# One order of matmuls for every block of a weight product

## The chip, the cores and the metric

The kernel runs on one core of a Trainium2 chip. The metric is the device time of one execution in microseconds (us), as the median of several timed runs. Beside the timed runs there is one profiled execution with a trace, from which all durations of single instructions come.

## The reference, cut to what matters

One layer of a decoder for 256 tokens of 2048 features, all in float32. The input is normalised, projected to ten pieces, and goes through two mixers side by side: latent attention with 16 heads, and a short causal convolution with gates. Both are projected, merged by sigmoid gates, and projected once more.

```python
h = _rmsnorm(x, pre_norm_g)
proj = jnp.einsum('bsd,de->bse', h, w_in)
(q_a, c_kv, k_rope, z_mla, c_in, b_gate, c_gate, z_conv, g_mla, g_conv) = jnp.split(proj, cuts, axis=-1)
q = jnp.einsum('bsr,re->bse', _rmsnorm(q_a, q_a_norm_g), w_q_b)
kv = jnp.einsum('bsr,re->bse', _rmsnorm(c_kv, kv_a_norm_g), w_kv_b)
...
attn = _causal_mla_attention(q_nope, q_rope, k_nope, k_rope, v)
attn = attn.reshape(b, s, MLA_WIDTH) * jax.nn.silu(z_mla)
y_mla = jnp.einsum('bse,ed->bsd', attn, w_o_mla)
u = c_gate * c_in
conv = sum(conv_w[k] * u_pad[:, k:k + s] for k in range(CONV_K))
y_conv = jnp.einsum('bse,ed->bsd', b_gate * conv * jax.nn.silu(z_conv), w_o_conv)
merged = jax.nn.sigmoid(g_mla) * y_mla + jax.nn.sigmoid(g_conv) * y_conv
out = jnp.einsum('bsd,de->bse', merged, w_out)
x = x + _rmsnorm(out, post_norm_g)
```

## The kernel before

Every float32 weight and every activation is split into two parts of 12 bits (float32r): a high part and the rest. A product of two such operands is taken as three products: high x high, high x rest, rest x high.

**The stream of weights.** `plan` lists units of [128, 2048] in the order of their use. `load_raw` brings a unit in on SP's queue, three units ahead. `split_unit` cuts it in two halves of 1024 columns; for each, `split_act` (L202 to L204) lets ScalarE write the high part `whi` and VectorE subtract it from the raw values into the rest `wlo`. There are five buffers of each. `take` hands out pieces of a unit, and before that calls `ahead`, which issues the loads and splits to come.

**The weight products.** The activations lie as `both`: 256 tokens' high parts and, beside them, their 256 rests, so one matmul with 512 columns multiplies a high weight part by both, and one with 256 columns multiplies the weight's rest by the high parts. This pair is `halves` (L196 to L200). It adds up over the contracted features in one PSUM bank of [128, 512]; at the end of a block `whole` (L311) adds the bank's two halves: ScalarE copies the right half out (`half`), and VectorE adds it to the left. A block of `project` (L320) has 16 pairs, a block of `narrow` (L430) 4. Four banks (`mm`) take turns. The products of two activations (scores, values) and the last projection (`out_products`, with `product`, L189) don't use `halves`.

**The stages.** First the latent query `qa` (four banks side by side, each pair goes to each bank in turn), then the latent keys and values `ckv` in four blocks, then `kr`. Beside them run the norms: the sums of squares go through a matmul with ones (`ss_...`, L289), GpSimd raises the mean to the power -1/2 (`r_...`, L295), VectorE puts it on a diagonal (`dg_...`, L299), and another matmul spreads it over all partitions (`rb_...`, L306). GpSimd (POOL) also computes the rotary angles in a long row of small steps (`tables`, L334 to L350). Then come 16 heads: in each, five blocks (`z`, `cg`, `ci`, `b`, `c`) beside the attention of the head, and the queries, keys and values (`qn`, `kn`, `qr`, `vv`) of the next two heads. Then 16 rounds of the output stage, with two gate blocks `g` and two blocks `y` each, and at last the shared output projection, its norm, the residual and the store.

**What sets the order.** Each engine has one queue. The code gives an order of issue, but the kernel is built with a scheduler that orders the instructions of each engine by its own estimate of their times:

```python
    with tile.TileContext(nc, schedule_with_timeline_sim=True) as tc:
        tile_layer(tc, *args)
```

Of the kernel before, what the change touches and what calls it, by code (L numbers as in the profile page):

```python
# [19 lines left out]
S = 256  # L20
NT = S // P
D = 2048
# [13 lines left out]
UNIT = 2048  # L36
HALF = UNIT // 2

# Column blocks of the packed small parameters: per-feature vectors, feature 128 k + p at [p, k].
PV = {}  # L40
_at = 0
for _name, _n in (
# [35 lines left out]
def tile_layer(ctx: ExitStack, tc: tile.TileContext, xt, x, pos, pvec, post_g, wqa, wi, wkr, wqk, wrv, wom, woc, wout, out):  # L78
# [3 lines left out]
    wpool = ctx.enter_context(tc.tile_pool(name="wpool", bufs=1))  # L82
    psum = ctx.enter_context(tc.tile_pool(name="psum", bufs=1, space=PSUM))

# [1 line left out]
    plan = []  # L86

    def add(ap, width=UNIT):
# [14 lines left out]
    order = []  # L103
    for h in range(H):
        g, second = divmod(h, HG)
# [81 lines left out]
        return psum.tile([P, 512], F32, name=name, tag=tag, bufs=bufs)  # L187

    def product(ps, a, b, first, last):  # L189
        # ps += a.T @ b, each operand in its two parts  # L190
        (ah, al), (bh, bl) = a, b
        nc.tensor.matmul(ps, ah, bh, start=first, stop=False)  # L192
        nc.tensor.matmul(ps, ah, bl, start=False, stop=False)  # L193
        nc.tensor.matmul(ps, al, bh, start=False, stop=last)  # L194

    def halves(ps, w, both, first, last):  # L196
        # both [128, 512]: 256 columns' parts side by side; ps[:, :256] + ps[:, 256:] += w.T @ columns
        order = ((w[0], 2 * S), (w[1], S)) if first else ((w[1], S), (w[0], 2 * S))
        for i, (a, n) in enumerate(order):
            nc.tensor.matmul(ps[:, :n], a, both[:, :n], start=first and i == 0, stop=last and i == 1)  # L200

    def split_act(hi, lo, src):  # L202
        nc.scalar.activation(hi, src, AF.Copy)  # L203
        nc.vector.tensor_tensor(lo, src, hi.bitcast(F32), op=ALU.subtract)  # L204

# [1 line left out]
    pv = const.tile([P, PV_N], F32, name="pv")  # L207
    nc.scalar.dma_start(out=pv[:, :], in_=pvec)

# [21 lines left out]
    cos_t = const.tile([P, S], F32, name="cos_t")  # L231
    sin_t = const.tile([P, S], F32, name="sin_t")

# [1 line left out]
    main = ctx.enter_context(ExitStack())  # L235
    hp = main.enter_context(tc.tile_pool(name="hp", bufs=1))
    x_both = hp.tile([P, KD, 2 * S], F32R, name="x_both")
# [7 lines left out]
    qa = bp.tile([P, KR, 2 * S], F32R, name="qa")  # L245
    ckv = bp.tile([P, KR, 2 * S], F32R, name="ckv")
    kr = bp.tile([P, 2, S], F32R, name="kr")
    # before the heads fill them: x, then the rotary angles; the latents, squares, sums, row norms
    xs = at_f
    angles = [at_f[:, H - 1 - i, :] for i in range(5)]  # L250
    lat_f = {"qa": cv_f[:, :KR, :], "ckv": cv_f[:, KR : 2 * KR, :]}
# [5 lines left out]
    def temp(name, shape=(P, S), dt=F32, bufs=2, tag=None):  # L257
        return bp.tile(list(shape), dt, name=name, tag=tag or name.rstrip("0123456789_"), bufs=bufs)

# [1 line left out]
    def x_chunk(i, j, pieces):  # L261
        n = 4 // pieces
        ks = slice(4 * i + n * j, 4 * i + n * (j + 1))
# [7 lines left out]
        )  # L271
        return a, b

# [1 line left out]
    def squares(name, chunks):  # L275
        # [128, 256]: sums of squares over the features of each partition
        acc = acc_f[name]
        for i, src in enumerate(chunks):
            nc.scalar.activation(sq_f, src, AF.Square)
            part = temp("f")[:, :] if i else acc  # L280
            nc.vector.reduce_sum(part, sq_f.rearrange("p k t -> p t k"), axis=mybir.AxisListType.X)
            if i:
                nc.vector.tensor_tensor(acc, acc, part, op=ALU.add)
        return acc
# [22 lines left out]
        nc.scalar.activation(r, rb[:, :S], AF.Copy)  # L307
        return r

# [1 line left out]
    def whole(dst, ps):  # L311
        # dst = ps[:, :256] + ps[:, 256:]
        t = temp("half")
        nc.scalar.activation(t[:, :], ps[:, S:], AF.Copy)
        nc.vector.tensor_tensor(dst, ps[:, :S], t[:, :], op=ALU.add)
# [8 lines left out]
            halves(ps, w(k, P), both[:, k, :], k == 0, k == KD - 1)  # L324
        return ps

# [1 line left out]
    def tables():  # L328
        pi = angles[4].bitcast(I32)
        nc.scalar.dma_start(out=pi, in_=pos.to_broadcast([P, S]))  # L330
        y, n1, n2, r = angles[:4]
        v = nc.gpsimd
        nc.vector.tensor_copy(y[:, :], pi)
        v.tensor_scalar(r[:, :], y[:, :], col("freq"), None, op0=ALU.mult)  # L334

        def less(r, n, c):
            # r -= n c, the product exact
            v.tensor_scalar(y[:, :], n[:, :], c, None, op0=ALU.mult)  # L338
            v.tensor_tensor(r[:, :], r[:, :], y[:, :], op=ALU.subtract)

        inv = 1.0 / (2.0 * math.pi)
        big, small = 1.5 * 2.0**38, 1.5 * 2.0**23
        v.tensor_scalar(y[:, :], r[:, :], inv, None, op0=ALU.mult)
        v.tensor_scalar(n1[:, :], y[:, :], big, big, op0=ALU.add, op1=ALU.subtract)
        v.tensor_tensor(n2[:, :], y[:, :], n1[:, :], op=ALU.subtract)
        v.tensor_scalar(n2[:, :], n2[:, :], small, small, op0=ALU.add, op1=ALU.subtract)
        for w, c in TERMS:
            less(r, (n1, n2)[w], c)
        v.tensor_scalar(n1[:, :], r[:, :], inv, small, op0=ALU.mult, op1=ALU.add)
        v.tensor_scalar(n1[:, :], n1[:, :], small, None, op0=ALU.subtract)  # L350
        for c in COARSE:
            less(r, n1, c)
        lim = float(np.nextafter(np.float32(math.pi), np.float32(0)))
        nc.vector.tensor_scalar(r[:, :], r[:, :], lim, -lim, op0=ALU.min, op1=ALU.max)
        nc.vector.scalar_tensor_tensor(y[:, :], r[:, :], -1.0, r[:, :], op0=ALU.mult, op1=ALU.max)
        nc.scalar.activation(n2[:, :], r[:, :], AF.Sin)
        nc.scalar.activation(cos_t[:, :], y[:, :], AF.Sin, bias=hpi[:, :], scale=-1.0)
        nc.vector.tensor_scalar(sin_t[:, :], n2[:, :], col("sign"), None, op0=ALU.mult)

    def rope(src, dst):  # L360
        # rows 0-31, 64-95: first halves; 32-63, 96-127: second halves
        a, b = temp("rp_a", bufs=1), temp("rp_b", bufs=1)
        nc.vector.tensor_tensor(a[:, :], src, cos_t[:, :], op=ALU.mult)
        for q in range(4):
            i, o = slice(32 * q, 32 * q + 32), slice(32 * (q ^ 1), 32 * (q ^ 1) + 32)
            nc.vector.tensor_tensor(b[o, :], src[i, :], sin_t[i, :], op=ALU.mult)
        nc.vector.tensor_tensor(dst, a[:, :], b[:, :], op=ALU.add)

# [1 line left out]
    def times_rows(dst):  # L370
        n = dst.shape[1]
        nc.vector.tensor_tensor(dst, dst, r_x[:, :].unsqueeze(1).to_broadcast([P, n, S]), op=ALU.mult)
# [48 lines left out]
        rope(kr_f, kr_f)  # L421
        split_act(kr[:, 0, :], kr[:, 1, :], kr_f)

# [1 line left out]
    def pair(name, shape, bufs=1):  # L425
        return [temp(f"{name}_{n}", shape, F32R, bufs, tag=f"{name}_{n}") for n in ("hi", "lo")]

# [22 lines left out]
    def group_b(g):  # L450
        qr, vv = temp("qr", (P, HG, S), F32R), pair("vv", (P, NT, HG * DV), 2)
        w = take(u_grp[g][1])
        f = narrow(f"qr{g}", w, 0, qa)
        rope(f[:, :], f[:, :])
        for j in range(HG):
            # both parts in one contraction: the first where the head's rows are, the second in the other rows
            own, other = (slice(DR * i, DR * i + DR) for i in (j, 1 - j))
            split_act(qr[own, j, :], qr[other, j, :], f[own, :])
        for t in range(NT):
            ps = bank(f"vv{g}_{t}", **({} if g else {"tag": ("o", "tp")[t], "bufs": 1}))  # L460
            for k in range(KR):
                c = [ckv[:, k, o + t * P : o + (t + 1) * P] for o in (0, S)]
                product(ps[:, :S], c, w(2 + k, HG * DV), k == 0, k == KR - 1)
            split_act(vv[0][:, t, :], vv[1][:, t, :], ps[:, :S])
        groups[g] += [qr, vv]

    def scores(h):
        # queries 0-127 by keys 0-127, in two addends; queries 128-255 by keys 0-255
        qn, kn, qr, _ = groups[h // HG]
        j = h % HG  # L470
        sc = bank(f"sc{h}", tag="sc", bufs=1)
# [32 lines left out]
        return p  # L504

    def turn(h, p):
        # keys 0-127 by queries 0-255; keys 128-255 by queries 128-255
        tp = bank(f"tp{h}", tag="tp", bufs=1)
        for b in range(3):
            nc.tensor.transpose(tp[:, b * P : (b + 1) * P], p[:, b * P : (b + 1) * P], ident[:, :])  # L510
        pt = temp("pt", (P, 2, 3 * P), F32R, 1)
        split_act(pt[:, 0, :], pt[:, 1, :], tp[:, : 3 * P])
        return pt
# [21 lines left out]
        return s  # L535

    def values_next(h):
        # this head's share of the next group
        g, second = divmod(h, HG)
        if g + 1 < NG:  # L540
            (group_b if second else group_a)(g + 1)
# [40 lines left out]
            values_next(h)  # L582
            values(h, turn(h, p), sz)

# [1 line left out]
    bstack.close()  # L586
    cp = main.enter_context(tc.tile_pool(name="cp", bufs=1))
    bp = cp
# [24 lines left out]
        split_act(m_both[:, d, :S], m_both[:, d, S:], m[0][:, :])  # L613
    main.close()

# [1 line left out]
    op = ctx.enter_context(tc.tile_pool(name="op", bufs=1))  # L617
    xr = op.tile([P, NT, D], F32, name="xr")
    og = op.tile([P, NT, D], F32, name="og")
# [21 lines left out]
    part = op.tile([P, NT], F32, name="part")  # L641

    def row_norm(t):
        # part: the squares of the first three blocks of columns, over D, plus eps
        ss = op.tile([P, 1], F32, name=f"fss{t}")
        nc.vector.scalar_tensor_tensor(
            ss[:, :], ssq[:, t, 3:4], 1.0 / D, part[:, t : t + 1], op0=ALU.mult, op1=ALU.add
# [30 lines left out]


def _cols(w):  # L680
    # [K, n 128] -> [n, 128, K]: block n's rows of 128 contracted features, side by side
    k, n = w.shape
    return np.ascontiguousarray(
        w.reshape(k // P, P, n // P, P).transpose(2, 1, 0, 3)
    ).reshape(n // P, P, k)
# [82 lines left out]
```

## Time and profile before

| | us |
|---|---|
| timed runs, median of 3 | 1084.33 |
| timed runs, lowest and highest | 1084.27, 1085.43 |
| profiled execution, span from its first to its last instruction | 1083.1 |
| TensorE matmuls busy in it | 1064.9 |
| VectorE busy | 785.4 |
| ScalarE busy | 599.1 |
| GpSimd busy | 47.4 |

The page gives the profiled execution by its span alone; what lies around the span is in the timed runs and not in the profile. Matmuls overlap in the records, and their ends are modelled, so the time that one matmul costs in a stream is read from the start of it to the start of the next. A line such as L200 is that of a helper, so groups are told apart by the names of the tiles: `g<-x_both,whi` writes the bank `g` from the activations and a high weight part. The idle time of TensorE is in the list of waits, by the matmul that waited and what released it.

### The profile page before, as it was taken

The page shows a single profiled execution, that of the slowest core. Times are in us where ns is not written, and L with a number is a line of the kernel's source. Part 1 is how long each engine was busy: PE and PEld are TensorE (multiplying, and loading weights), DVE is VectorE, ACT ScalarE, POOL GpSimd, SP SyncE. Part 2 cuts the span into 40 slices and gives each one's busy share as a digit, 9 for nine tenths or more (in the row PEclk, how much of TensorE's full clock was granted, in tenths as well). Part 3 has the DMA queues.
Part 4 walks back from the last instruction along what each step waited for, and adds up shares of the span by engine and source line. Part 5 has one row for each costly group of instructions (what it writes and reads, how often), then busy time and mean ns, then how long its engine had stood idle before and what let it go on. Part 6 is the DMA issues. An engine that isn't in the chain of part 4 may idle for free.

```text
span 1083.1 us, 15562 instructions
## 1 busy us (share of the span) xinstructions
PE 1064.9 (98%) x6056; PEld 927.0 (86%) x6056; DVE 785.4 (73%) x1260; ACT 599.1 (55%) x937; POOL 47.4 (4%) x70
## 2 busy tenths in 40 slices
PE   8999999999999999999999999999999999999997
PEld 7877888888888888888888888888888888888885
DVE  6899897877877878778787786656566565665562
ACT  7557566665656656566555674444444444444450
POOL 0591000000000000000000000000000000000000
PEclk9999999999999999999999999999999999999999
DMA  8544554454545545545545545555555555556652
GB/s 312 203 162 156 185 177 165 160 211 165 194 160 181 194 154 193 189 153 188 177 179 179 187 161 198 193 194 180 177 188 194 194 179 178 188 194 264 218 179 78
DMA packets 31610, 199.89 MB, mean 185 GB/s; under 512 B 3632, under 2 KB 5296, under 8 KB 9264
## 3 DMA queue, kind: packets, MB, share of 16 engines
q1 hardware_dynamic: 30960, 195.57, 51.2%
q10 hardware_dynamic: 576, 3.31, 0.8%
q8 instruction: 48, 0.79, 0.3%
q14 instruction: 26, 0.21, 0.0%
HBM read 196.78 MB, written 2.10 MB: 184 GB/s over the span
## 4 chain that ended last, share of the span: by engine, by line
PE 90%; DVE 3%; POOL 3%; issue 2%; DMA 1%; ACT 0%; SPq 0%; POOLq 0%; DVEq 0%; ACTq 0%
PE y L200 17%; PE g L200 17%; PE c L200 8%; PE b L200 8%; PE cg L200 8%; PE z L200 8%; PE ci L200 8%; PE out L194 2%; PE out L193 2%; PE out L192 2%; PE kn L200 2%; PE qn L200 2%; DMA raw<-wqa_dram 1%; POOL at_f L338 1%; PE qr L200 1%
## 5 line engine op out<-in xcount | busy, mean ns | idle before, releaser
L204 DVE TENSOR_TENSOR wlo<-raw,whi 128x1024 fp32r<-128x1024 f32 (+1 forms) x372 | 448.0, 1208 | 150.7 <-ACT whi L203 141.7
L203 ACT ACTIVATE whi<-raw 128x1024 fp32r<-128x1024 f32 (+1 forms) x374 | 386.2, 1035 | 202.3 <-PE y L200 39.3
L200 PE MATMUL g<-x_both,whi 128*128 128x512 f32 x512 | 181.1, 398 | 0.0
L200 PE MATMUL g<-x_both,wlo 128*128 128x256 f32 x512 | 138.6, 281 | 0.0
L200 PEld LDWEIGHTS g<-x_both,whi 128*128 128x128 f32 x512 | 95.3, 188 | 21.0
L200 PEld LDWEIGHTS g<-x_both,wlo 128*128 128x128 f32 x512 | 96.7, 189 | 2.7
L200 PE MATMUL b<-x_both,whi 128*128 128x512 f32 x256 | 94.3, 406 | 0.0
L200 PE MATMUL y<-at_both,whi 128*128 128x512 f32 x256 | 91.8, 398 | 0.0
L200 PE MATMUL cg<-x_both,whi 128*128 128x512 f32 x256 | 91.8, 398 | 0.0
L200 PE MATMUL y<-cv_both,whi 128*128 128x512 f32 x256 | 91.8, 398 | 0.0
L200 PE MATMUL ci<-x_both,whi 128*128 128x512 f32 x256 | 91.4, 397 | 0.0
L200 PE MATMUL c<-x_both,whi 128*128 128x512 f32 x256 | 91.2, 395 | 0.0
L200 PE MATMUL z<-x_both,whi 128*128 128x512 f32 x256 | 91.1, 396 | 0.0
L200 PE MATMUL b<-x_both,wlo 128*128 128x256 f32 x256 | 69.7, 283 | 0.0
L200 PE MATMUL y<-at_both,wlo 128*128 128x256 f32 x256 | 69.3, 281 | 0.0
L200 PE MATMUL y<-cv_both,wlo 128*128 128x256 f32 x256 | 69.3, 281 | 0.0
L200 PE MATMUL cg<-x_both,wlo 128*128 128x256 f32 x256 | 69.3, 281 | 0.0
L200 PE MATMUL c<-x_both,wlo 128*128 128x256 f32 x256 | 69.2, 281 | 0.0
L200 PE MATMUL z<-x_both,wlo 128*128 128x256 f32 x256 | 69.1, 280 | 0.0
L200 PE MATMUL ci<-x_both,wlo 128*128 128x256 f32 x256 | 68.8, 279 | 0.0
L200 PEld LDWEIGHTS b<-x_both,whi 128*128 128x128 f32 x256 | 48.7, 190 | 10.0
L200 PEld LDWEIGHTS y<-cv_both,whi 128*128 128x128 f32 x256 | 48.2, 188 | 10.5
(235 smaller groups left out, 1979.8 us busy)
## 6 DMA issues: line engine op xcount, KB each, us to landing
raw<-wi_dram SPq DMA_DIRECT2D x116, 1024.0 KB, 4.8
raw<-wom_dram SPq DMA_DIRECT2D x16, 1024.0 KB, 4.8
raw<-woc_dram SPq DMA_DIRECT2D x16, 1024.0 KB, 4.8
raw<-wout_dram SPq DMA_DIRECT2D x16, 1024.0 KB, 4.9
raw<-wqk_dram SPq DMA_DIRECT2D x8, 1024.0 KB, 4.8
raw<-wrv_dram SPq DMA_DIRECT2D x8, 768.0 KB, 4.3
raw<-wqa_dram SPq DMA_DIRECT2D x8, 256.0 KB, 4.5
raw<-wqa_dram SPq DMA_DIRECT2D x4, 512.0 KB, 8.0
```

The lines of the kernel that those rows point to most:

```text
L192: nc.tensor.matmul(ps, ah, bh, start=first, stop=False)
L193: nc.tensor.matmul(ps, ah, bl, start=False, stop=False)
L194: nc.tensor.matmul(ps, al, bh, start=False, stop=last)
L200: nc.tensor.matmul(ps[:, :n], a, both[:, :n], start=first and i == 0, stop=last and i == 1)
L203: nc.scalar.activation(hi, src, AF.Copy)
L204: nc.vector.tensor_tensor(lo, src, hi.bitcast(F32), op=ALU.subtract)
L338: v.tensor_scalar(y[:, :], n[:, :], c, None, op0=ALU.mult)
```

## The change

Only `halves` changes. Before, the first pair of a block has the matmul of 512 columns first and that of 256 second, and all later pairs have them the other way round. After, every pair has 512 first and 256 second. The first matmul of a block must in both cases be the one of 512 columns, since it starts the accumulation in the whole bank; the last is now one of 256 columns, where it was one of 512.

```diff
     def halves(ps, w, both, first, last):
-        # both [128, 512]: 256 columns' parts side by side; ps[:, :256] + ps[:, 256:] += w.T @ columns
-        order = ((w[0], 2 * S), (w[1], S)) if first else ((w[1], S), (w[0], 2 * S))
-        for i, (a, n) in enumerate(order):
+
+        for i, (a, n) in enumerate(((w[0], 2 * S), (w[1], S))):
             nc.tensor.matmul(ps[:, :n], a, both[:, :n], start=first and i == 0, stop=last and i == 1)
```

The changed file also has its comments taken out, and all lines behind this place stand one line higher (L200 becomes L199). No other code differs, but the scheduler places the instructions of all engines anew.

## The prediction

> **What bounds the kernel now.** I read the page from the top: the busy shares, then the chain that ended last.
>
> ```profile
> span 1083.1 us, 15562 instructions
> PE 1064.9 (98%) x6056; PEld 927.0 (86%) x6056; DVE 785.4 (73%) x1260; ACT 599.1 (55%) x937; POOL 47.4 (4%) x70
> PE 90%; DVE 3%; POOL 3%; issue 2%; DMA 1%; ACT 0%; SPq 0%; POOLq 0%; DVEq 0%; ACTq 0%
> ```
>
> TensorE matmuls are 98% of the span and 90% of the chain. The busy share alone would not prove that TensorE works without pause, since ends of matmuls are modelled. So I went to the waits of TensorE, which is the complete list (us in total, times, longest):
>
> ```profile
> PE rb_qa L306 <- DVE dg_qa L299: 2.6, 1, 2.6
> PE rb_ckv L306 <- DVE dg_ckv L299: 2.6, 1, 2.6
> PE qa L200 <- DVE wlo L204: 2.1, 2, 1.1
> PE idle L230 <- POOL ones L217: 1.1, 1, 1.1
> PE vv L192 <- DVE cg L315: 0.7, 1, 0.7
> PE rb_x L306 <- DVE dg_x L299: 0.6, 1, 0.6
> PE qa L200 <- ACT whi L203: 0.4, 1, 0.4
> ```
>
> Seven groups, 10.1 us in all, and every one of them lies in the first 140 us (the last is vv; its place, 138.66 us, is in the chain row quoted below). From there to the end nothing makes TensorE wait. So two questions decide the change: does a block of matmuls take another time in the new order, and what happens to the waits of the first 140 us.
>
> **The change, part by part.** *The matmul stream.* A block of `project` or `narrow` is a run of pairs, one matmul of 512 columns with the first part of a weight (whi) and one of 256 with the second (wlo). Before, the first pair is 512, 256 and all later pairs 256, 512; so at the seam of two blocks two 512s stand together, and then two 256s. After, 512 and 256 alternate throughout. No matmul is added or removed. Here is one block and its two seams in the timeline (start, duration):
>
> ```profile
> 901.83 0.62 PE L200 MATMUL g<-x_both,whi 128*128 128x512 f32 x2
> 902.30 0.40 PE L200 MATMUL g<-x_both,wlo 128*128 128x256 f32 x2
> 902.53 0.40 PE L200 MATMUL g<-x_both,whi 128*128 128x512 f32 x1
> 902.76 0.28 PE L200 MATMUL g<-x_both,wlo 128*128 128x256 f32 x1
> 902.88 0.40 PE L200 MATMUL g<-x_both,whi 128*128 128x512 f32 x1
> ...
> 907.48 0.40 PE L200 MATMUL g<-x_both,whi 128*128 128x512 f32 x1
> 907.72 0.39 PE L200 MATMUL y<-at_both,whi 128*128 128x512 f32 x1
> 907.94 0.40 PE L200 MATMUL y<-at_both,wlo 128*128 128x256 f32 x2
> 908.18 0.40 PE L200 MATMUL y<-at_both,whi 128*128 128x512 f32 x1
> ```
>
> Durations overlap, so I use starts. Alternating: from 902.53 to 907.48 are 14 pairs, 4.95 us, 0.3536 us a pair; a 256 takes 0.12 (902.76 to 902.88) and a 512 0.23 to 0.24. Around the seam: 512, 512, 256, 256 take 902.53 - 901.83 = 0.70 us, and again 908.18 - 907.48 = 0.70. The same four in alternation are two pairs, 0.707 us. So a seam costs 0.007 us more after, and rounding of the starts to 0.01 could make that zero. The blocks are 4 qa, 4 ckv, 16 x 5 in the heads, 16 x 4 in the output stage, and 8 x 5 short ones for queries and keys: 192 seams at most. That is 192 x 0.007 = 1.3 us at one end, 0 at the other; many seams in the heads are interrupted by score matmuls anyway, so I take the middle, **+0.7 us**.
>
> *The norm of the latents in the head of the kernel.* The scheduler places instructions by its own estimate, so a new order of matmuls moves other work. The programs as built differ in the heads' first stretch thus (count of weight matmuls before each norm matmul):
>
> ```
>             before                              after
> ss_qa       after 8 of z                        after 21 of z
> rb_qa       after 23 of cg                      after 9 of ci      (18 later)
> ss_ckv      after 13 of ci                      after 31 of ci     (18 later)
> rb_ckv      after 20 of b                       after 5 of c       (17 later)
> r_qa  on POOL                                   two table steps later
> r_ckv on POOL                                   one table step later, the last one
> ```
>
> rb_qa and rb_ckv are the two largest waits above. The timeline of TensorE and of POOL around them:
>
> ```profile
> 70.96 0.68 PE L306 MATMUL rb_qa<-dg_qa,ones 128*128 128x128 f32 x4 [2.62 <-DVE dg_qa L299]
> 85.40 0.68 PE L306 MATMUL rb_ckv<-dg_ckv,ones 128*128 128x128 f32 x4 [2.60 <-DVE dg_ckv L299]
> ```
> ```profile
> 70.01 0.72 POOL L339 TENSOR_TENSOR at_f<-at_f 128x256 f32<-128x256 f32 x1
> 70.82 0.90 POOL L338 TENSOR_SCALAR at_f<-at_f 128x256 f32<-128x256 f32 x1
> 71.81 0.74 POOL L339 TENSOR_TENSOR at_f<-at_f 128x256 f32<-128x256 f32 x1
> ...
> 81.30 0.91 POOL L338 TENSOR_SCALAR at_f<-at_f 128x256 f32<-128x256 f32 x1
> 82.85 1.63 POOL L295 TENSOR_TENSOR r_ckv<-v_ckv,mhalf 128x2 f32<-128x2 f32 x1 [0.65 <-DVE v_ckv L293]
> 84.45 0.72 POOL L339 TENSOR_TENSOR at_f<-at_f 128x256 f32<-128x256 f32 x1
> ```
>
> POOL works through the rotary tables in a row, and r_qa and r_ckv are queued among them. At rb_qa: the weights' 18 matmuls that now go ahead are 9 pairs, 9 x 0.3536 = 3.2 us of cover; r_qa comes two table steps later, 71.81 - 70.01 = 1.8 us. The wait of 2.6 becomes 2.6 + 1.8 - 3.2 = 1.2. At rb_ckv: one table step ahead of r_ckv takes from 82.21 (81.30 + 0.91) to about 83.1, against a start at 82.85 now: 0.25 us later, since POOL waited 0.65 there. Over both waits TensorE idled 5.2 us; after, 17 matmuls more (3.0 us) are done by then: 5.2 + 0.25 - 3.0 = 2.5. **A lead of 2.7 us** when rb_ckv is over.
>
> *The clock behind the wait.* The stretches just behind rb_ckv, with the granted clock in the sixth value:
>
> ```profile
> 86.00:88.00 2.00, 2.00 (x9) 1.75 (x9) 2.00 (x4) 1.73 (x3) 0.00 (x0) 0.60 0.99 418
> 88.00:90.00 2.00, 2.00 (x8) 1.62 (x7) 1.96 (x6) 1.25 (x5) 0.00 (x0) 0.55 0.03 12
> ```
>
> At 0.60 and 0.55, these 4 us did 1.2 + 1.1 = 2.3 us of full-clock work: 1.7 us lost, after an idle time of 2.6; the same wait at rb_qa was not followed by it. A wait cut to at most 2.5, probably shared between two places, need not bring it: up to **1.7 us** more, a lead of 4.4.
> By the Trainium skill ("TensorE: Matmul & The Clock Gate", Part 1) the gate closes after an idle window of about 3.4 us, free-running. By that rule 2.6 us should not have closed it, and here it did; the measurement decides. By the rule alone the 1.7 us would be lost in neither kernel, and the lead would be 2.7.
>
> *What is late next.* The lead is worth something only if the operands are there. VectorE (third value):
>
> ```profile
> 70.00:80.00 10.00, 9.04 (x55) 8.07 (x56) 9.89 (x15) 4.69 (x10) 9.15 (x12) 1.00 0.48 174
> 80.00:90.00 10.00, 7.41 (x35) 6.15 (x35) 9.35 (x20) 5.94 (x11) 4.43 (x4) 0.83 0.30 107
> 90.00:100.00 10.00, 10.00 (x62) 8.89 (x62) 9.96 (x22) 6.40 (x13) 0.10 (x1) 1.00 0.45 145
> 100.00:120.00 20.00, 20.00 (x122) 17.70 (x121) 19.80 (x39) 15.44 (x29) 0.00 (x0) 1.00 0.61 218
> ```
> ```profile
> 97.40 0.42 DVE L204 TENSOR_TENSOR ckv<-cv_f,ckv 128x256 fp32r<-128x256 f32 x1
> ```
> ```profile
> 98.45 1.17 PE kn L200 x7
> 138.66 0.39 PE vv L192
> ```
>
> Between 70 and 120 us VectorE is idle for 0.11 + 0.65 + 0.04 + 0.20 = 1.0 us in all. It makes the second parts of the weights, the parts of ckv that the key product kn reads (ready at 97.82, read from 98.45), and the drains of the banks, and none of that work goes away. So TensorE can be earlier by that 1.0 us, at most by 1.0 + 0.6 (the 0.6 between 97.82 and 98.45), and the rest of the lead turns into waits at kn, at the first scores or at head 1's z. I take **-1.0 us** (ends 0 and -1.6). The wait of 0.7 at vv (138.66) then meets a VectorE that has caught up or not: 0 to -0.7, I take **-0.4**.
>
> *At nothing.* The qa blocks now ask for whi first, which may shorten the 2.1 us of waits for wlo; but rb_qa and rb_ckv come from POOL's table chain, not from TensorE's start, so what is gained there idles at rb_qa (if that cover fell, up to -2.1). A whi buffer comes free one 256 earlier and a wlo buffer one 512 later, 0.24 us; no row shows VectorE waiting for TensorE, and this stays far from mattering. The new order also groups ScalarE's work so that 21 table loads stand in the program instead of 33:
>
> ```profile
> L533 ACT ACT_TABLE_LOAD x16 | 20.5, 1283 | 0.3
> ```
>
> 12 x 1.28 = 15 us of ScalarE saved, on an engine that is 55% busy and 0% of the chain. SP's order of transfers is the same in both.
>
> *Sum.* +0.7 - 1.0 - 0.4 = -0.7 us, so the profiled execution's 1083.1 becomes 1082.4. The median of the timed runs, 1084.33, lies 1.2 us above the span, which I take for what lies around it; 1084.33 - 0.7 = **1083.6 us**. A measurement of this kernel (1084.27 to 1085.43) can tell about 0.2%, 2.2 us, from no change.
>
> **The rivals.** *VectorE does not hold TensorE.* If the new order hands over operands in time, the whole lead of 4.4 and the vv wait count: 1084.33 - 4.4 - 0.4 + 0.7 = 1080.2. For it: VectorE's 4 us next to POOL are slow ones that other neighbours may speed up. Against it: 19.80 busy of 20. If the slow clock comes back at the shortened wait, 1.7 less remains: 1081.9, still faster by 0.2%. Chance 0.22.
>
> *VectorE's new queue makes TensorE wait for longer than the lead.* Place: 90 to 125 us, where keys, values, scores and head 1's z come close together, with four banks that only VectorE's adds set free. If an add or a split that TensorE needs stands behind two or three weight splits that it does not need, both engines end up waiting in turn. It decides once the waits there pass 4.4 us, the lead; one wait more of the size of rb_qa's, 2.6, gives 1084.33 + 2.6 + 0.7 = 1087.6. For it: no slack on VectorE. Against it: in the trace no wait of TensorE stands in this stretch at all. Chance 0.15.
>
> *The seam is not free.* If the first 512 of a block, now behind a 256, waits for its weights:
>
> ```profile
> L200 PEld LDWEIGHTS g<-x_both,whi 128*128 128x128 f32 x512 | 95.3, 188 | 21.0
> ```
>
> 188 ns of load behind a slot of 120 would leave 0.07 us x 192 = 13 us: 1097. Against it: 15 of 16 pairs already have a 512 behind a 256, at 0.3536 a pair. Chance 0.03. That the change did nothing at all falls within the forecast.
>
> **How the numbers follow.** Forecast 0.60, inside 0.2%; faster 0.22, slower 0.15 + 0.03 = 0.18. The range starts at the first rival, 1080.2, and ends where every unknown goes against the forecast: no gain in the head, +1.3 at the seams, and the 1.1 us by which the highest timed run exceeds the median, 1084.33 + 2.4 = 1086.7. The two slower rivals, 0.18, are left out.
>
> **What would show it.** Right: pairs at 0.353 across seams; the waits at rb_qa and rb_ckv together near 2.5 instead of 5.2; no stretch at 0.6 clock, or one that costs nothing; new waits of TensorE on VectorE between 90 and 125 us of some 3 us in all; none after 140. Wrong: a block in the output stage that takes 5.70 us or more, any wait after 140 us, or no waits between 90 and 125 (first rival).

## The result, and the profile after

The median went from 1084.33 us to 1086.39 us (13 runs, 1084.95 to 1088.31). The ratio is 1.0019, with an interval of 1.0011 to 1.0026: a small loss of 2.1 us, where a gain of 0.7 was forecast. The profiled execution took 1086.54 us, its span is 1084.7.

The head of the page of the kernel after, and its chain by engine:

```profile
span 1084.7 us, 15683 instructions
PE 1066.3 (98%) x6056; PEld 929.8 (86%) x6056; DVE 774.9 (71%) x1260; ACT 582.7 (54%) x925; POOL 48.9 (5%) x70
PE 88%; POOL 4%; DVE 3%; issue 2%; DMA 2%; SPq 0%; ACT 0%; POOLq 0%; DVEq 0%; ACTq 0%
```

As many matmuls as before and nearly the same shares: this page doesn't tell what happened. The list of TensorE's waits does (total, times, longest; the row left out is that of the first matmuls, 1.1 us as before):

```profile
PE rb_qa L305 <- DVE dg_qa L298: 2.7, 1, 2.7
PE z L199 <- DVE f L314: 2.4, 1, 2.4
PE kn L199 <- DVE ckv L203: 1.4, 1, 1.4
PE rb_ckv L305 <- DVE dg_ckv L298: 1.3, 1, 1.3
...
PE sc L474 <- DVE kn L203: 1.0, 1, 1.0
PE qa L199 <- ACT whi L202: 0.6, 1, 0.6
```

rb_qa waits as long as before, rb_ckv half as long; the waits at qa shrank from 2.5 to 0.6 us and those at vv (0.7) and rb_x (0.6) are gone; z, kn and sc wait, 4.8 us together, which did not wait at all. At qa little was gained: in this execution TensorE itself was slow there, with four 512s from 8.20 to 9.90 us, 0.43 us each, where one before takes 0.23 (8.13 to 8.36), so it asked for its operands later. The places of the four largest in the timeline of TensorE:

```profile
73.34 0.68 PE L305 MATMUL rb_qa<-dg_qa,ones 128*128 128x128 f32 x4 [2.68 <-DVE dg_qa L298]
86.38 0.68 PE L305 MATMUL rb_ckv<-dg_ckv,ones 128*128 128x128 f32 x4 [1.32 <-DVE dg_ckv L298]
96.39 0.47 PE L199 MATMUL kn<-ckv,whi 128*128 128x512 f32 x1 [1.37 <-DVE ckv L203]
112.79 0.50 PE L199 MATMUL z<-x_both,whi 128*128 128x512 f32 x1 [2.41 <-DVE f L314]
```

Head 1's z is the first matmul of a new bank. The timelines of VectorE ahead of it, first after, then before:

```profile
109.72 0.42 DVE L203 TENSOR_TENSOR kn<-f,kn 128x256 fp32r<-128x256 f32 x1
110.05 0.41 DVE L362 TENSOR_TENSOR rp_a<-f,cos_t 128x256 f32<-128x256 f32 x1
110.48 1.71 DVE L365 TENSOR_TENSOR rp_b<-f,sin_t 32x256 f32<-32x256 f32 x4
112.22 0.42 DVE L314 TENSOR_TENSOR f<-qn,half 128x256 f32<-128x256 f32 x1
```

```profile
109.52 0.42 DVE L315 TENSOR_TENSOR f<-qn,half 128x256 f32<-128x256 f32 x1
109.85 0.41 DVE L363 TENSOR_TENSOR rp_a<-f,cos_t 128x256 f32<-128x256 f32 x1
110.28 1.71 DVE L366 TENSOR_TENSOR rp_b<-f,sin_t 32x256 f32<-32x256 f32 x4
```

The add of the queries' bank (`f<-qn,half`) sets free the bank that z needs. Before, it stood ahead of the rotation of group 0's queries (`rope`); after, the scheduler put it behind the rotation's first five instructions, 0.4 + 1.7 = 2.1 us, and TensorE stood for 2.4. The windows of the kernel after from there on (the sixth value is the granted clock):

```profile
112.00:114.00 2.00, 1.21 (x5) 1.10 (x6) 1.97 (x4) 0.69 (x2) 0.00 (x0) 0.77 0.53 218
114.00:116.00 2.00, 2.00 (x8) 1.71 (x8) 1.87 (x6) 1.52 (x4) 0.00 (x0) 0.50 0.03 8
116.00:118.00 2.00, 2.00 (x12) 1.73 (x11) 1.69 (x5) 1.37 (x3) 0.00 (x0) 0.87 0.00 0
```

The slow clock that stood behind rb_ckv before stands behind this wait now: 0.46 + 1.0 + 0.26 = 1.7 us lost from 112 to 118, as much as before. It is no saving, only moved.

Starts of the same matmuls in the two timelines, in us:

| | before | after | difference |
|---|---|---|---|
| head 1's first z | 110.78 | 112.79 | +2.0 |
| head 2's first z | 147.75 | 150.26 | +2.5 |
| first g of the output stage | 625.47 | 627.11 | +1.6 |
| end of the span | 1083.1 | 1084.7 | +1.6 |

So the loss arises before 150 us; 0.9 of it is given back in the heads, and the output stage, 360 us long, adds next to nothing. In the output stage a row of the chain with 64 matmuls stands for two blocks, 32 pairs. First one row before, then three after:

```profile
659.43 11.29 PE y L200 x64
```

```profile
649.70 11.00 PE g L199 x63
660.70 11.31 PE y L199 x64
672.01 11.30 PE g L199 x64
```

That nearly nothing turned out to be the most instructive part, as the first experiment showed.

### The profile page after: what moved, and what is told of

The parts are those of the page before. It is cut to its first block, busy times and chain, and to the rows that moved or that the text cites. A ratio compares the mean times of both kernels' runs of the same rounds, so it can differ in the third digit from the quotient of the medians.

```text
span 1084.7 us, 15683 instructions
## 1 busy us (share of the span) xinstructions
PE 1066.3 (98%) x6056; PEld 929.8 (86%) x6056; DVE 774.9 (71%) x1260; ACT 582.7 (54%) x925; POOL 48.9 (5%) x70
## 4 chain that ended last, share of the span: by engine, by line
PE 88%; POOL 4%; DVE 3%; issue 2%; DMA 2%; SPq 0%; ACT 0%; POOLq 0%; DVEq 0%; ACTq 0%
PE y L199 17%; PE g L199 17%; PE z L199 8%; PE b L199 8%; PE c L199 8%; PE ci L199 8%; PE cg L199 8%; PE out L192 2%; PE out L194 2%; PE out L193 2%; PE qn L199 2%; PE kn L199 2%; DMA raw<-wqa_dram 2%; POOL at_f L337 1%; POOL at_f L338 1%
## 5 line engine op out<-in xcount | busy, mean ns | idle before, releaser
L199 PE MATMUL g<-x_both,whi 128*128 128x512 f32 x512 | 181.3, 398 | 0.0
L199 PE MATMUL g<-x_both,wlo 128*128 128x256 f32 x512 | 143.6, 281 | 0.0
L199 PEld LDWEIGHTS g<-x_both,whi 128*128 128x128 f32 x512 | 96.1, 188 | 23.6
L199 PEld LDWEIGHTS g<-x_both,wlo 128*128 128x128 f32 x512 | 96.7, 189 | 0.1
L199 PE MATMUL z<-x_both,whi 128*128 128x512 f32 x256 | 91.9, 400 | 2.4 <-DVE f L314 2.4
L199 PE MATMUL b<-x_both,whi 128*128 128x512 f32 x256 | 92.4, 403 | 0.0
L199 PE MATMUL y<-cv_both,whi 128*128 128x512 f32 x256 | 91.1, 398 | 0.0
L199 PE MATMUL y<-at_both,whi 128*128 128x512 f32 x256 | 91.1, 398 | 0.0
L199 PE MATMUL c<-x_both,whi 128*128 128x512 f32 x256 | 90.8, 396 | 0.0
L199 PE MATMUL ci<-x_both,whi 128*128 128x512 f32 x256 | 90.5, 395 | 0.0
L199 PE MATMUL cg<-x_both,whi 128*128 128x512 f32 x256 | 90.3, 394 | 0.0
L199 PE MATMUL z<-x_both,wlo 128*128 128x256 f32 x256 | 72.6, 284 | 0.0
L199 PE MATMUL ci<-x_both,wlo 128*128 128x256 f32 x256 | 72.0, 281 | 0.0
L199 PE MATMUL y<-cv_both,wlo 128*128 128x256 f32 x256 | 71.9, 281 | 0.0
L199 PE MATMUL y<-at_both,wlo 128*128 128x256 f32 x256 | 71.9, 281 | 0.0
L199 PE MATMUL c<-x_both,wlo 128*128 128x256 f32 x256 | 71.9, 281 | 0.0
L199 PE MATMUL b<-x_both,wlo 128*128 128x256 f32 x256 | 71.9, 281 | 0.0
L199 PE MATMUL cg<-x_both,wlo 128*128 128x256 f32 x256 | 71.8, 280 | 0.0
L199 PEld LDWEIGHTS z<-x_both,whi 128*128 128x128 f32 x256 | 48.8, 191 | 14.1 <-issue 2.7
L199 PEld LDWEIGHTS y<-cv_both,whi 128*128 128x128 f32 x256 | 48.1, 188 | 11.9
```

## The experiments

My theory after the comparison: the loss is VectorE's new queue in the first heads, and the seams are as good as free. The kernels before that ran beside the experiments had medians of 1084.5 to 1084.8 us.

**The new order in the output stage alone.** Up to there all engines have the order of the kernel before.

```diff
+    uniform = [False]
-        order = ((w[0], 2 * S), (w[1], S)) if first else ((w[1], S), (w[0], 2 * S))
+        order = ((w[0], 2 * S), (w[1], S)) if first or uniform[0] else ((w[1], S), (w[0], 2 * S))
...
+    uniform[0] = True
     for d in range(KD):
```

> The old order up to the end of the heads, the new order only in the 64 blocks of the output stage; every engine's order of instructions is that of the kernel before up to that stage. Theory (the loss is VectorE's queue in head 0, and the order of the matmuls itself costs about 5 ns a block): 64 x 0.005 = +0.3 us, ratio 1.0003, no new wait of TensorE. Rival (each seam costs, the 2.06 us are spread over 152 long blocks): 64/152 of it, +0.9 us, ratio 1.0008.

Measured: 1078.65 us (1077.85 to 1079.03), ratio 0.9946 (0.9934 to 0.9959). Neither theory expected a gain. Its chain in the output stage:

```profile
658.02 11.09 PE y L202 x64
```

11.09 us for 32 pairs is 346.6 ns a pair; 11.31 is 353.4 (346.7 and 353.3 from 700 to 980 us in the two traces). The granted clock is 1.00 throughout in both. From its first g to the first matmul of the last projection the stage takes 355.0 us here, and 361.3 in the kernels before and after. The kernel with the change has almost the same order there, and yet its rows are slow. So a stream of alternating pairs has two paces, and something decides which. In the heads both paces come up, in all kernels; score matmuls interrupt the stream there all the time.

**The new order in the head alone** (latents and heads 0 and 1, by `uniform[0] = h < 2`; the rest as before).

> The new order only in the latent blocks and in heads 0 and 1, the old order behind them; every engine's order is that of the changed kernel up to there. Theory (VectorE's queue in head 0): waits of TensorE at kn, sc and z of some 5 us in all as in the changed kernel, and the whole loss or more: +2.0 to +2.6 us, ratio 1.0019 to 1.0024. Rival (each seam costs): 18 of 152 long blocks, +0.25 us, ratio 1.0002.

Measured: 1087.24 us (1085.57 to 1089.21), ratio 1.0025 (1.0015 to 1.0035). Its waits of 2.7 (rb_qa), 2.4 (z), 1.4 (kn) and 1.0 (sc) are those of the kernel with the change. The loss lies here. From head 0's first z to head 1's, with the same matmuls between them, TensorE takes 52.6 us in the trace before and 55.5 here and in the trace after; the other traces agree (51.7 to 52.7 us in seven with the old order there, 54.8 to 56.5 in seven with the new one and the rotation on VectorE). What the change does in the later heads makes up for 0.9 us of it, as the table above shows.

**The rotation off VectorE.** The change, and group 0's rotation of the queries is computed by GpSimd.

```diff
-    def rope(src, dst):
+    def rope(src, dst, e=nc.vector):
...
-        rope(f[:, :], f[:, :])
+        rope(f[:, :], f[:, :], nc.vector if g else nc.gpsimd)
```

> The changed kernel, but the rotation of the first group's queries (six steps, 2.5 us) goes to GpSimd, so that it no longer stands on VectorE ahead of the step that frees the bank of head 1's z. Theory: the wait at z (2.4 us) shrinks to under 0.8 and the slow clock behind it (about 1.7 us) does not come: 2 to 4 us less than the changed kernel, ratio to the kernel before 0.998 to 1.000. Rival (each seam costs, the waits in the head are covered): as the changed kernel, 1.002.

Measured: 1083.45 us (1080.58 to 1083.97), ratio 0.999 (0.9981 to 0.9999), 2.9 us less than the change alone. A row of its waits, and one of its windows:

```profile
PE z L200 <- DVE f L315: 1.0, 1, 1.0
```

```profile
114.00:116.00 2.00, 2.00 (x14) 1.77 (x14) 1.86 (x5) 2.00 (x6) 0.00 (x0) 1.00 0.00 0
```

The wait at z went from 2.4 to 1.0, and no slow clock follows it. The waits at kn and sc stay. That is 1.4 of the 2.9 us. Another 0.6 comes later: from head 2's first z to the output stage this kernel takes 476.25 us (144.90 to 621.15), the change 476.85 (150.26 to 627.11). The rest, 0.9, may be the slow clock behind z, but that is not shown: this profile is of the fastest run, 1080.58 against a median of 1083.45, and has no slow stretch anywhere in the heads. So the rotation on VectorE costs 2.9 us; how much of that the change brought about, a later run tells.

**All matmuls of 512 columns of a block first, then all of 256** (the loop of qa in the old order):

```diff
+    def parts(ps, ws, boths):
+        for i, n in ((0, 2 * S), (1, S)):
+            for k, (w, both) in enumerate(zip(ws, boths)):
+                nc.tensor.matmul(ps[:, :n], w[i], both[:, :n], ...)
```

> Per block all matmuls of 512 columns first, then all of 256 (projections and the short blocks; the latent queries keep the old order). Theory (a 512 behind a 512 and a 256 behind a 256 are cheaper than alternation, as the last projection's 0.229 us and the values' 0.118 show): 16 x 0.347 = 5.55 us a block against 5.65, 0.1 us x 162 blocks, -16 us, ratio 0.985, less what new waits in head 0 give back. Rival (only the number of columns counts): 5.65 a block, ratio 1.000 within the head's 0.2%.

Measured: 1081.98 us (1081.26 to 1082.99), ratio 0.9977 (0.9968 to 0.9986), far less than expected. A row of its output stage and the largest of its waits:

```profile
661.79 11.13 PE y L205 x64
```

```profile
PE z L205 <- DVE f L323: 4.3, 1, 4.3
```

Grouped, 64 matmuls take 11.13: better than alternation at its slow pace, no better than at its fast one (11.09). And the head waits longer still.

**An extra matmul in the slow stream.** The change, and one matmul of 128, 256 or 64 columns into a spare bank, in the middle of a block of round 2. No other instruction moves.

```diff
+        if d == 2:
+            kick = bank("kick", tag="sm", bufs=1)
+            nc.tensor.matmul(kick[:, :128], m_both[:, 1, :P], m_both[:, 1, :128], start=True, stop=True)
```

> The changed kernel with one more matmul (128 columns, 0.06 us, its result unused) inside the first gate block of round 2 of the output stage; no other instruction moves on any engine. Theory (the alternating stream has two paces, 346.7 and 353.3 ns a pair, and keeps the one it has until something else passes through it): the pace behind the extra matmul may be the other one. If it is, some 880 pairs x 6.6 ns = 5.8 us less than the changed kernel, ratio to the kernel before 0.9965; if it falls back into the same pace, 1.0019. Rival (the pace is set by where buffers lie or by what the other engines do): 353.3 behind it as before it, 1.0019.

> As the run before, with 256 columns in the extra matmul. Theory of the two paces: at least one of the two sizes changes the pace to 346.7, ratio 0.9965 for it. Rival: 353.3 throughout, 1.0019.

> The kernel with the change and one extra matmul of 64 columns inside block g1 of round 2, nothing else moved; extra ones of 128 and of 256 columns left the pace at 353.3 ns. Theory A1 (where the stream lands depends on the length of what passes): 346.7 from 678 us on, 1086.4 - 5.9 = 1080.5 us. Theory A2 (a disturbed stream ends at 353.3 whatever passes): 353.3, 1086.5 us.

Measured: 1086.06 (ratio 1.0013, 1.0004 to 1.0022), 1087.09 (1.0018, 1.0009 to 1.0027) and 1086.99 us (1.0021, 1.0012 to 1.0029). None brought the stream to the fast pace.

**The same extra matmul in the fast stream** (128 columns, in the kernel with the new order in the output stage alone).

> The kernel with the new order only in the output stage, which ran there at 346.7 ns a pair, with the extra matmul of 128 columns in round 2. Theory of the two paces: it stays at 346.7 (ratio 0.995) or goes over to 353.3 from there on (0.9946 + 5.8 us, ratio 1.000). Rival (placement or neighbours): 346.7 throughout, 0.995.

Measured: 1084.55 us (1083.53 to 1085.58), ratio 0.9997 (0.9988 to 1.0006). Its chain around the extra matmul:

```profile
658.79 11.09 PE y L202 x64
669.89 7.85 PE g L202 x45
677.74 0.06 PE kick L606
677.80 3.35 PE g L202 x19
681.15 11.30 PE y L202 x64
```

One matmul of 0.06 us costs 5.9 us: from it on, every row takes 11.3, with all other instructions of all engines in the order of the fast kernel. So a stream can change its pace when something irregular passes, and that the fast kernel owed its pace to another placement is refuted.

**The rotation off VectorE, old order in the heads, new order in the output stage.**

> New order only in the output stage, and the rotation of the first group's queries on GpSimd. Theory (TensorE's waits in head 0 come from VectorE's queue): the kernel before has only 0.7 us of waits behind rb_ckv, so there is little to win: 0 to -1.5 us against the new order in the output stage alone, ratio 0.993 to 0.9946, if the output stage keeps its pace of 346.7. If the pace falls to 353.3: about 1.000. Rival (GpSimd's steps slow VectorE down): slower by 1 us, 0.9955.

Measured: 1077.5 us (1077.12 to 1077.92), ratio 0.9934 (0.9921 to 0.9946). This is 1.2 us less than the new order in the output stage alone, although in the old order the add stands ahead of the rotation; the wait of 0.7 at vv is gone. So of the 2.9 us that the rotation costs in the change, 1.2 were there before, and some 1.8 are due to the new order: most of the 2.1 us that the change lost.

**One block in the old order.** Block g1 of round 2, once in the fast stream, once in the slow stream of the change:

```diff
+            uniform[0] = (d, n) != (2, 1)
             whole(sg[:, :], project(ug, f"g{n}_{d}"))
```

> The kernel with the old order up to the end of the heads and the new one in the output stage, but one block of the output stage (g1 of round 2) in the old order: its two seams put two 256s together, and two 512s, with as many matmuls as before. Theory A (a stream keeps the pace in which it runs until something irregular passes, and an old seam is such a thing): the pace is 346.7 ns up to this block, at about 678 us, and 353.3 ns from there to the end of the output stage, and the time 1084.5 us, the same as with the extra matmul of 128 columns (1084.55). Theory B (one seam is not enough, or brings the stream back to where it was: the old order is slow in the output stage since each block pays for itself): one block of 5.65 us, then 346.7 again, 1078.8 us. About 1079 and a pace of 346.7 behind the block means that this seam does not flip it, which would leave open what does in the kernel before.

> The kernel with the change, but block g1 of round 2 in the old order (also the split of one weight unit behind it is placed a little differently). The stream comes to it at 353.3 ns a pair. Theory A1 (anything irregular lands the stream anew in one of the two paces, either way): the pace can go to 346.7 behind this block, and the time is then 1086.4 - 6.0 = 1080.4 us. Theory A2 (353.3 is the pace in which a disturbed stream ends, and only a clean start gives 346.7): it stays 353.3, 1086.4 us.

Measured: 1078.76 (ratio 0.9948, 0.9934 to 0.9962) and 1086.3 us (1.0016, 1.0007 to 1.0025). A single old block does nothing either way: the fast stream stays fast, the slow one slow. Its two seams are only halves of those of the kernel before, a pair of 256s at its start and a pair of 512s at its end.

**Two rounds in the old order** in the fast stream, with full seams (512, 512, 256, 256) between their eight blocks:

```diff
+        uniform[0] = d not in (2, 3)
```

> The kernel with the old order up to the end of the heads and the new one in the output stage, but rounds 2 and 3 of the output stage (eight blocks) in the old order, so that seven seams have the form 512, 512, 256, 256 of the kernel before. The stream comes in at 346.7 ns a pair. Theory C (this full seam, unlike the half seams of a single old block, puts the stream into 353.3 ns; that is why the output stage of the kernel before runs at it): inside the eight blocks the pairs take 353.3 ns. If it then stays so to the end, 1084.5 us; if the half seam that leaves them brings it back, 1078.65 + 8 x 0.1 = 1079.5 us, with 346.7 behind round 3. Theory D (the old seams do nothing to the pace, and before runs at 353.3 for what came ahead of the output stage): 346.7 inside the eight blocks too, 1078.7 us.

Measured: 1084.1 us (1083.44 to 1085.73), ratio 0.9996 (0.9987 to 1.0005). Its chain; round 2 begins at 669.17:

```profile
669.17 11.11 PE g L202 x64
680.28 11.30 PE y L202 x64
```

The first full seam, in the middle of the first row, leaves the pace fast; from the second one on the rows are slow, and they stay so to the end, behind round 3 too. So an old seam can change the pace, and the kernel before, with one at every block, runs its output stage slowly. The change takes them away. Why is its own stream slow then?

The streams of the output stage of the change and of the fast kernel differ at one place. In the change, the scheduler issues the first 512 of g1 of round 1 some fifteen matmuls early, in the middle of block g0. In the timeline of the kernel after, the row with x2 is that place:

```profile
651.97 0.28 PE L199 MATMUL g<-x_both,wlo 128*128 128x256 f32 x1
652.08 0.62 PE L199 MATMUL g<-x_both,whi 128*128 128x512 f32 x2
652.54 0.28 PE L199 MATMUL g<-x_both,wlo 128*128 128x256 f32 x1
```

There two 512s stand together. The row of 63 matmuls around it, shown above, took 11.00 us, between the 10.87 of the fast kernel's row of 63 at that place (shown below) and the 11.13 or so of 63 at the slow pace; all later rows are slow.

**That displacement by hand**, in the fast stream: the 512 of the ninth pair of one block stands behind the first pair.

```diff
+            if name == "g1_2" and k == 1:
+                nc.tensor.matmul(ps, w(8, P)[0], both[:, 8, :], start=False, stop=False)
+            if name == "g1_2" and k == 8:
+                nc.tensor.matmul(ps[:, :S], w(8, P)[1], both[:, 8, :S], start=False, stop=False)
+                continue
             halves(ps, w(k, P), both[:, k, :], k == 0, k == KD - 1)
```

> The kernel with the old order up to the end of the heads and the new one in the output stage (346.7 ns a pair throughout, 1078.65 us), and in one block, g1 of round 2, the 512 of its ninth pair stands fourteen matmuls early, behind the first pair: 512, 512 there, and 256, 256 where it is missing. That is the form in which the scheduler displaces one 512 in the kernel with the change. Theory (this displaced 512 throws the stream into the other pace): 346.7 up to about 677 us, 353.3 from there to the end, 1084.5 us. Rival (one displaced 512 does nothing, something else behind the head differs): 346.7 throughout, 1078.7 us.

Measured: 1084.5 us (1083.38 to 1085.25), ratio 0.9998 (0.9989 to 1.0006). L327 is the matmul put early, L329 the 256 that it left:

```profile
675.04 0.23 PE g L327
675.27 2.46 PE g L202 x14
677.74 0.12 PE g L329
...
680.33 11.31 PE y L202 x64
```

From there on the stream is slow, and VectorE, ScalarE and GpSimd have the order of the fast kernel: the matmul's place alone does it. But not every displaced 512 does. In the change and in the fast kernels alike, the first 512 of g0 of round 1 stands fifteen matmuls early, among those of the last y of round 0. This is the place in the kernel with the new order in the output stage alone:

```profile
644.37 0.24 PE g L202
644.60 2.55 PE y L202 x15
647.15 10.87 PE g L202 x63
```

Behind it the rows stay at 11.09. The starts, which the traces keep to the nanosecond, show a difference: the fast stream has two forms, one in which each 256 takes some 117 ns to the next start, one in which 113 and 118 take turns. The extra matmul, both displaced 512s that slowed the stream and the second full seam fell into the second form; the harmless displaced 512, the first full seam and the end of the single old block fell into the first. The start of the single old block fell into the second and did no harm. This is a pattern in eight cases, not a cause shown.

**The displacement taken out** of the change. With three of the subtractions at the start of the stage given to GpSimd, the scheduler does not displace that 512, and TensorE's order is otherwise that of the change, matmul by matmul. (VectorE's and ScalarE's differ around that place; in the run before they didn't.)

```diff
-            split_act(both[:, hs, :S], both[:, hs, S:], f[:, hs, :])
+            split_act(both[:, hs, :S], both[:, hs, S:], f[:, hs, :], nc.gpsimd if both is cv_both and h >= 12 else nc.vector)
```

> The kernel with the change, and the subtractions that make the last four of the second parts of cv_both (three instructions, at the start of the output stage) are on GpSimd in place of VectorE. With that the scheduler leaves the first 512 of g1 of round 1 in its place; the order on TensorE is otherwise that of the kernel with the change, matmul by matmul. Theory (the displaced 512 put the stream into 353.3): 346.7 from about 627 us to the end of the output stage, 1086.4 - 6.0 = 1080.4 us; the waits in the head stay (rb_qa 2.7, z 2.4, kn 1.4). Rival: the flip at 652 us comes without it, 1086.4 us; or a wait for the parts of cv_both, which GpSimd makes more slowly, and a time above that.

> The kernel with the change, group 0's rotation of the queries on GpSimd (1083.45 alone) and the three subtractions too. Theory (loss in the head and pace in the output stage are two separate things that add up): 1083.45 - 6.0 = 1077.5 us, like the best so far (1077.5, old order in the heads). Rival (pace not mended): 1083.4 us.

Measured: 1080.12 us (1076.89 to 1080.9), ratio 0.9955 (0.9942 to 0.9969), with the subtractions alone, and 1077.26 us (1075.43 to 1077.47), ratio 0.9925 (0.9912 to 0.9937), with the rotation on GpSimd as well. The first one's chain:

```profile
657.27 11.09 PE y L199 x64
```

Both came out within 0.3 us of the sums that were expected. The two effects are separate and add up: 6.3 us for one matmul's place, 2.9 for the rotation's. The last kernel has the lowest median of all, 7 us below the kernel before; it is the change, with VectorE relieved at two places. The kernel with the old order in the heads, the new one in the output stage and the rotation on GpSimd has 1077.5: with the rotation off VectorE, the new order in the heads is worth nothing that these runs can tell.

## Why the prediction was wrong, point by point

A gain of 0.7 us was forecast, and 2.1 us were lost. That the median still lies below the upper end of the range, 1086.7, is luck: this end was added up from no gain in the head, dear seams and the spread of the runs, without any loss behind VectorE, which is what came. The step that failed is the one on VectorE, -1.0 us: it let new waits behind VectorE take up TensorE's lead and no more, and they came to 4.8 us against a lead of 1.2.

**What bounds the kernel** held: TensorE, with all its waits before 140 us.

**The wait at rb_qa** was the first term that failed, in the order of time: 2.6 + 1.8 - 3.2 = 1.2 was forecast, 2.7 measured. In the timelines of VectorE, dg_qa starts at

```profile
72.46 0.93 DVE L298 TENSOR_SCALAR dg_qa<-ident,r_qa 128x128 f32<-128x128 f32 x2 [1.55 <-POOL r_qa L294]
```

after, and before at

```profile
70.08 0.93 DVE L299 TENSOR_SCALAR dg_qa<-ident,r_qa 128x128 f32<-128x128 f32 x2 [0.91 <-POOL r_qa L295]
```

That is 2.4 us later, not 1.8: GpSimd's table steps are not constant (one and the same step, of L337, takes 0.85 to 1.70 us in the trace after). And TensorE was through with its work ahead of it at 73.34 - 2.68 = 70.66, before at 70.96 - 2.62 = 68.34: 2.3 us later, not 3.2, since it had come to head 0's first z 0.9 us earlier (57.28, before 58.22). 2.6 + 2.4 - 2.3 is the 2.7. The forecast's table leaves out the norm matmul ahead of these, rb_x, which moved too. First before, then after:

```profile
50.33 0.68 PE L306 MATMUL rb_x<-dg_x,ones 128*128 128x128 f32 x4 [0.62 <-DVE dg_x L299]
```

```profile
51.03 0.66 PE L305 MATMUL rb_x<-dg_x,ones 128*128 128x128 f32 x4
```

From rb_x to head 0's first z TensorE has 41 matmuls before and 32 after. So the 18 matmuls of cover at rb_qa are only 9 if they are counted from rb_x, where TensorE was held up for GpSimd before: from rb_x to rb_qa it works 18.0 us before and 19.6 after. The shorter waits at qa don't explain it. In six traces with the change's order up to here they come to anything from 0.5 to 2.1 us, and rb_qa waits 2.7 in five of these and 3.7 in one. With rb_ckv the two waits are 4.0 against the 2.5 of the forecast; the lead from them was 1.2, not 2.7.

**The clock** was counted into the lead, 1.7 us, since the wait in front of it would be shorter. The slow stretch came behind the new wait at z instead; in other executions it stands elsewhere (last section). A cost that follows a wait should have been put to whatever wait was forecast next.

**The waits of 90 to 125 us** were the right mechanism at the right place with too small a size: kn, sc and z, as named, but 4.8 us in place of some 3. What failed was the sign of the sum: the forecast took these waits as the rest of the lead, so that they could at most use it up. They follow from the order of VectorE's queue and need no lead. That was the second rival, with a chance of 0.15. Its point of decision, 4.4 us of waits, was passed, and its price, 1087.6, is 1.2 us above the 1086.39. Its mechanism came true but for one thing: the add stood behind a rotation and not behind splits of weights. VectorE's order can be read from the two programs as built, next to TensorE's; I compared TensorE's and GpSimd's places only.

**The wait at vv** went, 0.7 us where 0.4 was taken, the middle of 0 and 0.7.

**The seams** were the largest miss, and hidden by the result. As a difference between rows at the same pace the term was right: 11.31 against 11.29 for two blocks, 0.01 a block, some 0.6 us in the output stage. But the 0.3536 us a pair, read from one block, was taken for what alternation costs. It is one of two paces. The old seams hold the output stage at the slow one, and without them it may run at 346.7 ns, worth 6 us. That the change didn't get it hangs on one displaced matmul.

**At nothing**: the 12 ScalarE table loads saved changed nothing that can be seen. **Around the span** lie 1.84 us, not 1.2.

Open is what in TensorE makes the two paces, and which disturbance moves it from one to the other. An extra 128, a displaced 512 and the second of two full seams took it from fast to slow; half seams, the first full seam and another displaced 512 did not; in long streams nothing that I tried took it back, while in the heads it goes both ways.

## What to carry to other kernels

With a scheduler, a new order on one engine is a new order on all: compare the queue of every engine that frees a bank or hands out an operand around each place where the bound engine will be early, not the bound engine's own. Read the pace of a stream of matmuls in several stretches and in blocks of some ten us, down to 1%; if it has two values, look at what passes where it changes. One irregular matmul can cost a hundred times its own duration. And a profile is of one execution: hold its time against the median of the runs, and its waits against other profiles with the same order, before a difference is divided among them.

## What the runs showed of the hardware that I had not expected

*Two paces.* Alternating matmuls of 512 and 256 columns in one order, at a granted clock of 1.00, run at 346.7 or at 353.3 ns a pair, and keep it for 300 us; one matmul of 0.06 us switches it. The Trainium skill ("TensorE: Matmul & The Clock Gate", Part 1, "Wait — 56ns, not 53.3ns?") gives a warm matmul its columns at 2.4 GHz and about 2.5 ns, an estimate of 325 ns for such a pair; both paces here lie above it.

*The clock behind a wait.* A wait of 2.4 us at z was followed by a clock of 0.5 in the kernel after. In the change with the subtractions on GpSimd the wait at z is as long, in its timeline

```profile
111.06 0.47 PE L199 MATMUL z<-x_both,whi 128*128 128x512 f32 x1 [2.40 <-DVE f L314]
```

and the clock stays at 1.00 behind it. In this execution the slow stretch stands behind rb_qa, after a wait of 2.0 us. Two of its windows:

```profile
72.00:74.00 2.00, 2.00 (x9) 1.80 (x8) 2.00 (x3) 1.75 (x4) 1.86 (x2) 0.50 0.00 0
114.00:116.00 2.00, 2.00 (x14) 1.75 (x13) 1.82 (x6) 1.10 (x3) 0.00 (x0) 1.00 0.00 0
```

So a wait of this length may or may not bring the slow clock, and the place changes from one execution to the next. In seven traces with the new order in heads 0 and 1 and the rotation on VectorE, such stretches, each worth 1.7 us, stand behind rb_qa in six and behind z in four, one or two to a trace. In seven traces with the old order there each has one, behind rb_ckv in three and behind rb_qa in four; in these four rb_ckv then waits 1.0 to 1.1 us and not 2.6, so most of the 1.7 us is not lost. What makes the spread of the runs stays open.
